# Expert 0's weights split during w_out; ranks, one-hots and slots in other places of TensorE's and VectorE's order

## The chip, the core and the metric

The kernel runs on one core of one Trainium2 chip. The metric is device time in microseconds (us) from the first to the last instruction, with what lies around them. TensorE multiplies; VectorE and ScalarE compute on tiles and empty TensorE's results out of PSUM; POOL (GpSimd) does some element work and issues the indirect transfers; SP issues the plain ones.

## What is computed

One layer of a hybrid trunk on 512 rows of 1024 columns: a norm, three token mixers, an output projection, a norm, then 16 experts in 4 groups, of which each row takes two, and a last norm. The change touches the stretch from the output projection to the first experts:

```
    return y @ w_out                                   # hybrid_mixer
    h = layer_norm(ALPHA * h + mix, ln1_g[l], ln1_b[l])
    ffn = grouped_moe(h, w_router, router_bias, ...)
...
    scores = jax.nn.sigmoid((t @ w_router))            # grouped_moe
    sel = (scores + router_bias).reshape(-1, N_GROUPS, EXPERTS_PER_GROUP)
    g_idx = argmax(sum of the two best sel of each group)
    e_idx = the two best experts of that group
    w_sel = scores at e_idx, divided by their sum
    h = silu(t @ w_gate[e]) * (t @ w_up[e])
    y = sum over a row's experts of w_sel * (h @ w_down[e])
```

## The kernel before

All large products run in three passes: a value is split into a rounded high half and the low half that is left over, and high*high, high*low and low*high are added up in PSUM. `split` makes the two halves of a raw weight page of 128 x 1024: a cast on ScalarE (L316), a subtraction on VectorE (L317). `mm3` (L332 to L334) issues the three products. SBUF is cut into pages of 4 KB per partition; `new` and `drop` take and free them, and a `Ring` hands out a fixed set of pages in turn.

The program is written as one list of instructions; a planner in the framework gives each engine its order by its own estimates. An instruction that is pinned (`pin`, or an engine wrapped as `Pinned`, all of which show as L144) keeps the written order among the pinned ones of its engine. `issue_after(i)` puts an instruction behind `i` on its engine. Engines run their orders strictly in sequence.

**w_out.** The 512 rows are four tiles, n = 0 to 3. Columns 0 to 511 are done for all tiles first; then columns 512 to 1023 tile by tile, TensorE pinned: four units u of six products (`wo_mm`). Between the units stand the router's steps of earlier tiles: transposes and products of `logits`, `scores`, the norm's `moments`, and `rows`, which finishes h1 and stores it to HBM (L1304). `half` adds the product to the residual (L1235) and takes the norm's sums.

**Routing.** `choose(n0, n1)` makes, for two tiles, the mask `Mb` of chosen experts (L1343) with some 20 small VectorE instructions; it returns `weigh`, which makes the routing weights in `rc` (L1355 to L1362). `ranks(n0, n1)` multiplies `Mb` with triangular matrices to get each row's place in its expert's list, adds it into `pos`, and makes the one-hot matrix `oh0` of expert 0 (L1375). `choose(0, 2)`, its `weigh` and `ranks(0, 2)` stand in tile 2 after unit 2; those of tiles 2 and 3 behind tile 3.

**Expert 0's input** is not gathered: `rows0(q, n0, n1)` multiplies tiles n0 to n1 - 1 of the residual with `oh0` into PSUM (L1382); `parts` splits the result. Tile 3 is normed late: a product with `ident` brings x*g into PSUM (L1294), one with the row of means adds the bias (L1295), and ScalarE scales it (L1296).

**Slots.** `slots_of(e0, e1)` makes for each expert a one-hot of 128 x 512 on VectorE (L1461), four products with `rc`, and from them the indices `gidx` and `sidx`; the function it returns (`rest`) makes the weights `wsl` in the same way. Other experts' input comes by an indirect transfer from HBM (`gather`, L1490), is transposed (`ex_in`, L1521) and split (L1513, L1514).

**Experts.** `weights(e)` loads six pages: four units of gate and up (two transfers of 256 KB each, L1504) and two of down (512 KB, L1506). `ex_up` is 24 products of 512 columns in four units, `ex_down` of the expert before follows it: the gate (L1534, L1535), two transposes (L1538), the split `mh` (L1541, L1542), 12 products, and the scatter to HBM (L1551). The split halves lie in rings `whs` and `wls` of three pages each; the raw pages in a ring of all that is free, 31.

Around the change the written order is: w_out's tile 3, `logits(1)`, `scores`, `rows`, `choose(2, 4)`, `rows0(0 and 1, 0, 2)`, `ranks(2, 4)`, the loads of experts 0 and 1, `rows0(0, 2, 4)`, slots of 1, `rows0(1, 2, 4)`, with the splits of expert 0's units 0 to 2 between them (`early`), the gather for expert 1, expert 0's 24 products, `weigh`, the rests, `slots(0)`, `slots(2, 3)`, `slots(4..7)`, `ex_in` of expert 1, its products.

## Time and profile before

| | us |
|---|---|
| median of three timed runs | 903.03 (901.21 to 904.04) |
| the profiled execution | 896.39 |
| its span, first to last instruction | 894.7 |
| TensorE busy in it | 829.8 |
| VectorE, ScalarE, POOL busy | 603.9, 442.9, 169.4 |

The times below are from the start of the span. Line numbers are those of the kernel before; L144 stands for every pinned instruction, which is told apart by its tiles. In a row of the timeline stand start, duration, engine, line, operation, what is written and read, the shape, the count, and in brackets how long the engine had stood idle and what released it. A matmul's duration is modelled and overlaps the next: six products of 512 columns take 1.64 us together, though each is shown with 0.39.

### The profile page before, as it was taken

What the parts mean: (1) busy time and instruction counts of PE and PEld (TensorE: products, weight loads), DVE (VectorE), ACT (ScalarE), POOL (GpSimd) and SP (SyncE); (2) the same over time, 40 slices, a digit from 0 to 9 for tenths busy, and PEclk for the clock granted to TensorE, in tenths of its full rate; (3) what the DMA queues carried; (4) which work ended last, traced back from release to release, by engine and by line L of the source; (5) the groups of instructions that cost most, each with busy time, mean ns of one, the idle gap of its engine ahead of it and who ended that gap; (6) DMA issues with size and microseconds to landing.
All of it is one profiled execution on the core that took longest, in us unless ns stands there. A gap on an engine that the chain in (4) does not pass through costs nothing. (4 is left out here: it accounts for less than half of the span.)

```text
span 894.7 us, 15185 instructions
## 1 busy us (share of the span) xinstructions
PE 829.8 (93%) x5860; PEld 694.0 (78%) x5860; DVE 603.9 (68%) x1104; ACT 442.9 (50%) x824; POOL 169.4 (19%) x197
## 2 busy tenths in 40 slices
PE   8989999999989999999999999999989699999950
PEld 5867778978987999988888888888767577777730
DVE  7775566777666646685834435445467999989958
ACT  6533466654556453556323323333214588888833
POOL 2550001440451330201000000000112122221132
PEclk9989999999999999999999999999999899999985
DMA  6512221022023122144434234247416999997043
GB/s 195 138 53 73 84 71 59 25 78 68 25 96 109 57 71 72 48 144 140 155 105 141 86 103 120 79 156 250 151 47 240 347 354 368 359 356 277 27 168 133
DMA packets 99999, 125.90 MB, mean 141 GB/s; under 512 B 12967, under 2 KB 86775, under 8 KB 99924
## 3 DMA queue, kind: packets, MB, share of 16 engines
q1 hardware_dynamic: 89344, 109.17, 36.7%
q10 hardware_dynamic: 6116, 7.48, 2.6%
q0 software_dynamic: 4464, 8.25, 2.4%
q8 instruction: 47, 0.77, 0.3%
q14 instruction: 28, 0.23, 0.1%
HBM read 118.21 MB, written 14.68 MB: 149 GB/s over the span
## 5 line engine op out<-in xcount | busy, mean ns | idle before, releaser
L317 DVE TENSOR_TENSOR rr<-ff,rr 128x1024 fp32r<-128x1024 f32 x148 | 183.8, 1248 | 115.9 <-ACT rr L316 113.5
L316 ACT CAST rr<-ff 128x1024 fp32r<-128x1024 f32 x150 | 156.9, 1054 | 168.1 <-PE ps L333 126.2
L332 PE MATMUL ps<-rh,rr 128*128 128x512 f32 x384 | 153.8, 400 | 0.0
L333 PE MATMUL ps<-rh,rr 128*128 128x512 f32 x384 | 150.7, 393 | 0.0
L334 PE MATMUL ps<-rh,rr 128*128 128x512 f32 x384 | 150.6, 392 | 0.0
L332 PE MATMUL ps<-rr,rh 128*128 128x256 f32 (+1 forms) x320 | 93.3, 292 | 0.6 <-DVE rh L144 0.6
L334 PE MATMUL ps<-rr,rh 128*128 128x256 f32 (+1 forms) x320 | 91.8, 288 | 0.8 <-issue 0.8
L333 PE MATMUL ps<-rr,rh 128*128 128x256 f32 (+1 forms) x320 | 91.4, 286 | 0.0
L332 PEld LDWEIGHTS ps<-rh,rr 128*128 128x128 f32 x384 | 72.6, 189 | 15.5 <-issue 0.8
L334 PEld LDWEIGHTS ps<-rh,rr 128*128 128x128 f32 x384 | 72.5, 189 | 15.4
L333 PEld LDWEIGHTS ps<-rh,rr 128*128 128x128 f32 x384 | 72.6, 189 | 14.2
L332 PEld LDWEIGHTS ps<-rr,rh 128*128 128x128 f32 x320 | 61.0, 191 | 2.6 <-issue 1.3
L334 PEld LDWEIGHTS ps<-rr,rh 128*128 128x128 f32 x320 | 60.9, 191 | 1.4 <-issue 0.8
L333 PEld LDWEIGHTS ps<-rr,rh 128*128 128x128 f32 x320 | 61.1, 191 | 0.2
L332 PE MATMUL ps<-rr,ro 128*128 128x512 f32 x120 | 48.5, 404 | 0.8 <-ACT ro L1513 0.7
L333 PE MATMUL ps<-rr,ro 128*128 128x512 f32 x120 | 48.3, 402 | 0.8 <-POOL rr L317 0.6
L334 PE MATMUL ps<-rr,ro 128*128 128x512 f32 x120 | 47.7, 398 | 0.6 <-DVE ro L1514 0.6
L1238 POOL TENSOR_TENSOR ff<-ff,ff 128x512 f32<-128x512 f32 x2 | 2.6, 1278 | 213.4 <-DVE ff L144 213.4
L334 PE MATMUL ps<-ro,rr 128*128 128x512 f32 x96 | 37.4, 389 | 0.0
L332 PE MATMUL ps<-ro,rr 128*128 128x512 f32 x96 | 37.3, 389 | 0.0
L333 PE MATMUL ps<-ro,rr 128*128 128x512 f32 x96 | 37.3, 389 | 0.0
L434 DVE SCALAR_TENSOR_TENSOR scr<-ps,vcol,scr 128x511 f32<-128x511 f32 (+2 forms) x36 | 26.7, 743 | 10.7 <-ACT scr L431 10.1
(576 smaller groups left out, 1676.6 us busy)
## 6 DMA issues: line engine op xcount, KB each, us to landing
ff<-in_w_in_dram SPq DMA_DIRECT2D x66, 512.0 KB, 3.4
ff<-in_w_gate_dram SPq DMA_DIRECT2D x47, 256.0 KB, 5.9
ff<-in_w_up_dram SPq DMA_DIRECT2D x47, 256.0 KB, 6.3
ff<-in_w_down_dram SPq DMA_DIRECT2D x19, 512.0 KB, 7.0
fh<-in_w_down_dram SPq DMA_DIRECT2D x10, 512.0 KB, 6.1
ff<-in_w_out_dram SPq DMA_DIRECT2D x8, 512.0 KB, 3.7
fh<-in_w_gate_dram SPq DMA_DIRECT2D x14, 256.0 KB, 6.0
fh<-in_w_up_dram SPq DMA_DIRECT2D x14, 256.0 KB, 7.3
```

The source lines that it names most:

```text
L316: S.copy(a, src)
L317: i = V.tensor_sub(b, src, a.bitcast(F32))
L332: TE.matmul(ps, w(0, k), h(0, k), start=start and k == k0, stop=False)
L333: TE.matmul(ps, w(0, k), h(1, k), start=False, stop=False)
L334: last = TE.matmul(ps, w(1, k), h(0, k), start=False, stop=stop and k == k1 - 1)
L434: V.scalar_tensor_tensor(y[:, sh:], ps[:, :T - sh], convw[:, j, j0:j0 + 1], y[:, sh:], op0=ALU.mult, op1=ALU.add)
L1238: G.tensor_mul(xg3[:, cs], t[:, cs], g1r[:, cs])
```

## The change

Expert 0's weights get six pages of their own and are loaded before the second half of w_out; two of its four units are split there into four new pages (`fr`, taken from the eight pages `fh`). `ranks(0, 2)` moves from tile 2 to tile 3. Behind w_out, `rows0` of tiles 0 and 1 is spread between the router's and the norm's steps of tile 3, which are now all pinned on TensorE. The casts of units 2 and 3 of expert 0 are free to run from `copied` on, their subtractions (`low`) keep the places of two `early`. `slots(2, 3)` and `weigh` go behind unit 2 of expert 0; the rests and `slots(0)` behind unit 1 of expert 1; `slots(4..7)` behind unit 1 of expert 2. The rings of split halves grow from three to five pages each. The functions `wsrc` and `weights` are the same as before, but for the argument `page`.

```diff
@@ -99,7 +99,12 @@
         def __init__(self, n, dt=F32, last=False):
             self.pages = [new((P, D), dt, last=last) for _ in range(n)]
             self.ids = [owner[id(a)][0] for a in self.pages]
-            self.i = 0
+            self.i, self.dt = 0, dt
+
+        def grow(self, n):
+            r = Ring(n, self.dt)
+            self.pages += r.pages
+            self.ids += r.ids
 
         def __call__(self, shape, dt=F32):
             self.i += 1
@@ -1182,7 +1187,8 @@
     branch(2, oB, gB, gla_norm, MB, w_br_b)
     drop(*hT[0], *hT[1])
     rh.close()
-    Pages("fh", 8, F32, side="right")
+    Pages("fr", 4, F32R, side="right")
+    Pages("fh", 4, F32, side="right")
 
 
     def rowload(a):
@@ -1235,7 +1241,7 @@
             W.tensor_add(t[:, cs], t[:, cs], psw)
             W.bn_stats(st[:, c], t[:, cs])
             if n == NT - 1:
-                G.tensor_mul(xg3[:, cs], t[:, cs], g1r[:, cs])
+                act[0] = G.tensor_mul(xg3[:, cs], t[:, cs], g1r[:, cs])
 
         def logits(c):
 
@@ -1243,8 +1249,8 @@
             ps = pst(pm)
             for k in range(4):
                 TE.transpose(ps[:, k * P:(k + 1) * P], t[:, (4 * c + k) * P:(4 * c + k + 1) * P], ident)
-            S.copy(hT1, ps)
-            yield
+            copied = S.copy(hT1, ps)
+            yield copied
             if n == NT - 1:
                 for k in range(4):
                     TE.matmul(psl[c][:, n * E:(n + 1) * E], hT1[:, k * P:(k + 1) * P], gwr[:, 4 * c + k], start=k == 0, stop=k == 3)
@@ -1284,16 +1290,19 @@
                 ms = nr0[:, 0, 0:2]
                 G.tensor_scalar(ms[:, 0:1], nm, 1.0, None, op0=ALU.mult)
                 G.tensor_scalar(ms[:, 1:2], mv[:, 1:2], LN_EPS, r[0], op0=ALU.add, op1=ALU.mult)
+                cs = [slice(c * T, (c + 1) * T) for c in range(2)]
+                psx = [pst(pp) for c in range(2)]
+                for c in range(2):
+                    TE.matmul(psx[c], ident, xg3[:, cs[c]], start=True, stop=False)
+                rows0(0, 1, 2)
                 ps = pst(pm)
                 TE.transpose(ps[:2, :P], ms, ident)
                 mr = sm.tile([P, P], F32, name="mr", tag="sq", bufs=2)[:2]
                 after(lambda: S.copy(mr, ps[:2, :P]))
+                rows0(1, 0, 1)
                 for c in range(2):
-                    cs = slice(c * T, (c + 1) * T)
-                    ps = pst(pp)
-                    TE.matmul(ps, ident, xg3[:, cs], start=True, stop=False)
-                    TE.matmul(ps, mr, gb2[:2, cs], start=False, stop=True)
-                    after(lambda: S.activation(t[:, cs], ps, AF.Copy, scale=r[0]))
+                    TE.matmul(psx[c], mr, gb2[:2, cs[c]], start=False, stop=True)
+                    after(lambda: S.activation(t[:, cs[c]], psx[c], AF.Copy, scale=r[0]))
             elif n:
                 W.scalar_tensor_tensor(t, t, m, g1r, op0=ALU.subtract, op1=ALU.mult)
                 W.scalar_tensor_tensor(t, t, r[0], b1r, op0=ALU.mult, op1=ALU.add)
@@ -1382,6 +1391,22 @@
                 TE.matmul(xps[q][:, c * P:(c + 1) * P], ah[n][:, (4 * q + c) * P:(4 * q + c + 1) * P], oh0[:, n],
                           start=n == 0 and c == 0, stop=n == NT - 1 and c == 3)
 
+    def wsrc(w, e):
+        return w[0, bass.ds(e, 1)].rearrange("o (k p) f -> p (o k) f", p=P)
+
+    def weights(e, page=None):
+
+        r = []
+        for u in range(6):
+            raw = (page or raws)((P, 2, T))
+            if u < 4:
+                for j, w in enumerate((w_gate, w_up)):
+                    nc.sync.dma_start(raw[:, :, 256 * j:256 * j + 256], wsrc(w, e)[:, 2 * u:2 * u + 2])
+            else:
+                nc.sync.dma_start(flat(raw), wsrc(w_down, e)[:, u - 4])
+            r.append(raw)
+        return r
+
     def wo_mm(n, u, w, ps):
         return mm3(ps, pairs(yT, slice(n * P, (n + 1) * P)), lambda b, k: w[b][:, k % 2], 2 * u, 2 * u + 2, u == 0, u == 3)
 
@@ -1398,6 +1423,8 @@
         lns[n][0](0, psw[n])
 
     ws = [wo_unit(1, u) for u in range(2)] + late
+    first = [weights(0, new)]
+    ready = []
     TE = Pinned(nc.tensor)
     for n in range(NT):
         ps = pst(pp)
@@ -1416,21 +1443,25 @@
                 lns[n - 1][3]()
             if u == 2 and n == 2:
                 choose(0, 2, V)()
+            if u == 2 and n == 3:
                 ranks(0, 2, V)
+            if u == 3 and n < 2:
+                ready.append(split(first[0][n], *(new((P, 2, T), F32R, at="fr") for _ in range(2)), pinned=True))
         lns[n][0](1, ps)
-    for _ in lns[3][1](1):
+    half, logits, scores, rows, _ = lns[3]
+    xps += [pst(pp) for _ in range(2)]
+    made = act[0]
+    W, TP = Pinned(V), TE
+    it = logits(1)
+    copied = next(it)
+    rows0(0, 0, 1)
+    for _ in it:
         pass
-    TE = nc.tensor
-    half, logits, scores, rows, _ = lns[3]
     scores()
     rows()
-    xps += [pst(pp) for _ in range(2)]
-    W, TP = Pinned(V), Pinned(nc.tensor)
     weigh = choose(2, 4, W)
-    for q in range(2):
-        rows0(q, 0, 2)
-    TE = TP
     ranks(2, 4, W)
+    rows0(1, 1, 2)
     drop(*x4)
     drop(*yT[0], *yT[1], g1r, b1r)
     for t in (raws, whs, wls):
@@ -1438,10 +1469,14 @@
     ry.close()
     Pages("fl", 8, F32)
     xTs, whs, wls = Ring(4, F32R), Ring(3, F32R), Ring(3, F32R)
+    for p in ready:
+        drop(*p)
+    whs.grow(2)
+    wls.grow(2)
     xgr, yos = Ring(3, last=True), Ring(2, last=True)
     ohp = new((P, 4, NT * P // 2), last=True).bitcast(BF)
     noh = [0]
-    drop(xg3, gb2, ohf, *ah)
+    drop(xg3, gb2, ohf, *first[0], *ah)
     raws = Ring(len(freed[F32]))
 
 
@@ -1481,7 +1516,8 @@
     xgs = []
     for i in range(3):
         t = xgr((P, D))
-        G.memset(t, 0.0)
+        with tc.issue_after(made.ins):
+            G.memset(t, 0.0)
         xgs.append(t)
 
     scats = []
@@ -1491,27 +1527,11 @@
             out=dst, out_offset=None, in_=h1d, in_offset=bass.IndirectOffsetOnAxis(ap=idx, axis=0),
             bounds_check=T - 1, oob_is_err=False)
 
...
 
     def parts(xT, q, ps, V=V):
         qs = slice(4 * q, 4 * q + 4)
         S.copy(flat(xT[0][:, qs]), ps)
-        V.tensor_sub(flat(xT[1][:, qs]), ps, flat(xT[0][:, qs]).bitcast(F32))
+        return V.tensor_sub(flat(xT[1][:, qs]), ps, flat(xT[0][:, qs]).bitcast(F32))
 
     def ex_in(xg):
         xT = [xTs((P, KD, P), F32R), xTs((P, KD, P), F32R)]
@@ -1522,11 +1542,19 @@
             parts(xT, q, ps)
         return xT
 
-    def ex_up(xT, raw, ready=(), e=0):
+    def ex_up(xT, raw, ready=(), e=0, hook={}):
         ps = pst(pp)
         for u in range(4):
-            w = ready[u] if u < len(ready) else split(raw[u], V=G if e == E - 1 and u == 3 else V)
+            if u < len(ready):
+                w = ready[u]
+            elif e == 1:
+                with tc.issue_after(act[0].ins), tc.issue_after(lows.ins):
+                    w = split(raw[u])
+            else:
+                w = split(raw[u], V=G if e == E - 1 and u == 3 else V)
             mm3(ps, lambda b, k: xT[b][:, k], lambda b, k: w[b][:, k % 2], 2 * u, 2 * u + 2, u == 0, u == 3)
+            if u in hook:
+                hook[u]()
         return ps
 
     def ex_down(ps, raw, wcol, sidx_col, m=2 * T, e=0):
@@ -1564,7 +1592,7 @@
 
     def fetch(e):
         wts = weights(e) if e > 1 else first[e]
-        if e % 4 == 1 and e < E - 4:
+        if e % 4 == 1 and 1 < e < E - 4:
             slots_of(e + 3, e + 7)()
         xg = xgs[e % 3]
         if e > 1:
@@ -1572,35 +1600,43 @@
         return wts, ex_in(xg)
 
 
-    first = [weights(0), weights(1)]
+    first.append(weights(1))
     xT = [xTs((P, KD, P), F32R), xTs((P, KD, P), F32R)]
-    ready = []
-
-    def early(u):
-
-        with tc.issue_after(act[0].ins):
-            ready.append(split(first[0][u], pinned=True))
+    for raw in first[0][2:4]:
+        w = whs((P, 2, T), F32R), wls((P, 2, T), F32R)
+        with tc.issue_after(copied.ins):
+            S.copy(w[0], raw)
+        ready.append(w)
+
+    def low(u):
+        W.tensor_sub(ready[u][1], first[0][u], ready[u][0].bitcast(F32))
 
     rows0(0, 2, 4)
-    rest = slots_of(1, 2, W, lambda: early(0))
+    rest = [slots_of(1, 2, W, lambda: low(2))]
     rows0(1, 2, 4)
     parts(xT, 0, xps[0], W)
-    early(1)
     gather(xgs[1], gidx[:, 1:2])
-    parts(xT, 1, xps[1], W)
-    early(2)
+    low(3)
+    lows = parts(xT, 1, xps[1], W)
     wts = first[0]
+
+    def slots23():
+        rest.append(slots_of(2, 4, W))
+        weigh()
+
+    def weights03():
+        with tc.issue_after(lows.ins):
+            rest.append(slots_of(0, 1))
+        for f in rest:
+            f()
+
+    hooks = [{2: slots23}, {1: weights03}, {1: lambda: slots_of(4, 8)()}] + [{}] * (E - 3)
     late = None
     for e in range(E):
         if e == E - 1:
             ex_down(*late, e=e - 1)
         TE = TP if e == 0 else nc.tensor
-        ps = ex_up(xT, wts, ready if e == 0 else (), e=e)
-        if e == 0:
-            weigh()
-            rest()
-            slots_of(0, 1, W)()
-            slots_of(2, 4, W)()
+        ps = ex_up(xT, wts, ready if e == 0 else (), e, hooks[e])
         if 0 < e < E - 1:
             ex_down(*late)
         late = ps, wts, wsl[:, e:e + 1], sidx[:, e:e + 1]
```

## Rows read from the trace of the kernel before

**Rows 1.** Page, part 1: busy us and share of each engine.

```profile
PE 829.8 (93%) x5860; PEld 694.0 (78%) x5860; DVE 603.9 (68%) x1104; ACT 442.9 (50%) x824; POOL 169.4 (19%) x197
```

**Rows 2.** Stage table: length; busy PE, PEld, DVE, ACT, POOL; clock, DMA share, GB/s.

```profile
636.00:642.00 6.00, 6.00 (x34) 4.46 (x32) 0.55 (x1) 1.43 (x3) 1.20 (x1) 1.00 0.00 1
...
658.90:662.10 3.20, 0.05 (x2) 0.06 (x3) 2.63 (x17) 0.63 (x2) 0.00 (x0) 0.97 0.28 114
662.10:666.00 3.90, 3.90 (x18) 3.32 (x19) 2.53 (x14) 0.00 (x0) 0.00 (x0) 0.58 0.01 2
666.00:673.70 7.70, 7.70 (x39) 5.72 (x39) 5.71 (x20) 0.80 (x2) 0.00 (x0) 1.00 0.06 24
673.70:688.50 14.80, 13.21 (x98) 10.23 (x96) 11.07 (x45) 5.84 (x9) 4.83 (x7) 1.00 0.81 283
688.50:694.20 5.70, 5.70 (x28) 4.52 (x28) 5.47 (x9) 3.75 (x4) 1.87 (x1) 1.00 0.64 210
694.20:703.70 9.50, 2.41 (x62) 1.93 (x58) 8.87 (x26) 2.71 (x3) 0.47 (x1) 0.78 1.05 383
703.70:714.40 10.70, 10.70 (x52) 9.07 (x49) 9.53 (x16) 7.19 (x10) 2.94 (x3) 0.88 0.90 323
714.40:724.40 10.00, 10.00 (x51) 8.12 (x50) 9.26 (x11) 8.69 (x13) 2.07 (x2) 1.00 0.98 317
724.40:734.40 10.00, 10.00 (x48) 7.85 (x47) 9.05 (x11) 8.60 (x13) 2.14 (x2) 1.00 1.06 386
734.40:845.00 110.60, 108.11 (x565) 85.78 (x563) 101.94 (x122) 93.16 (x131) 25.84 (x20) 1.00 0.82 292
```

**Rows 3.** Timeline, TensorE in w_out, tile 2 to tile 3.

```profile
662.05 0.20 PE L144 MATMUL ps<-Mb,SUb 128*128 128x16 bf16 x1 [3.15 <-DVE Mb L1343]
...
662.15 2.91 PE L144 MATMUL ps<-ro,ry 128*128 128x512 f32 x6
...
665.90 1.64 PE L144 MATMUL ps<-rr,ry 128*128 128x512 f32 x6
```

**Rows 4.** Timeline, end of w_out to expert 0's products.

```profile
672.03 1.67 PE L144 MATMUL ps<-ro,ry 128*128 128x512 f32 x6
...
681.21 0.19 DVE L144 SCALAR_TENSOR_TENSOR Mb<-scr,ru 128x32 bf16<-128x32 f32 x1
...
683.63 0.20 PE L144 MATMUL ps<-Mb,onb 128*128 128x16 bf16 x2
...
688.48 5.73 PE L144 MATMUL ps<-rr,ro 128*128 128x512 f32 x24
```

**Rows 5.** Timeline, TensorE from expert 0 to expert 1.

```profile
697.43 0.19 PE L144 MATMUL ps<-rc,fl 128*128 128x3 bf16 x2 [3.18 <-DVE rc L144]
...
703.67 1.95 PE L144 MATMUL ps<-ident,fl 128*128 128x128 f32 x8
```

**Rows 6.** Timeline, then line L1490 at 686 to 700: first gather, landing.

```profile
688.12 2.25 POOL L1490 DMA_INDIRECT fl<-h1d,gidx  x1 [9.72 <-DVE ro L144]
...
DMA to landing us min/median/max: 7.6/7.6/7.6
```

**Rows 7.** Page, part 5: VectorE's subtraction of a split.

```profile
L317 DVE TENSOR_TENSOR rr<-ff,rr 128x1024 fp32r<-128x1024 f32 x148 | 183.8, 1248 | 115.9 <-ACT rr L316 113.5
```

**Rows 8.** Timeline, two weight transfers and the last cast; landing of L1506.

```profile
584.03 0.37 SPq L1504 DMA_DIRECT2D ff<-in_w_gate_dram  x1
...
813.66 0.33 SPq L1506 DMA_DIRECT2D ff<-in_w_down_dram  x1
...
856.12 1.05 ACT L316 CAST rr<-ff 128x1024 fp32r<-128x1024 f32 x1 [0.76 <-PE ps L334]
...
DMA to landing us min/median/max: 5.1/6.5/8.0
```

**Rows 9.** Waits, 720 to 862: us in total, times, longest.

```profile
ACT rr L316 <- PE ps L334: 19.7, 39, 1.4
...
PEld ps L332 <- ACT mh L1541: 3.6, 5, 1.4
```

More of the change, by code (lines that the diff above doesn't have):

```diff
@@ L1492, in gather @@
             bounds_check=T - 1, oob_is_err=False)
-    def wsrc(w, e):
-        return w[0, bass.ds(e, 1)].rearrange("o (k p) f -> p (o k) f", p=P)
-    def weights(e):
-        r = []
-        for u in range(6):
-            raw = raws((P, 2, T))
-            if u < 4:
-                for j, w in enumerate((w_gate, w_up)):
-                    nc.sync.dma_start(raw[:, :, 256 * j:256 * j + 256], wsrc(w, e)[:, 2 * u:2 * u + 2])
-            else:
-                nc.sync.dma_start(flat(raw), wsrc(w_down, e)[:, u - 4])
-            r.append(raw)
-        return r
     def parts(xT, q, ps, V=V):
```

## The prediction

> **What bounds the kernel now.** I read the page first: TensorE is busy in 93% of the span [rows 1], so only a stretch in which it stands still can give much. The stage table (busy time in chosen stretches) then shows where that is [rows 2]: apart from the start and the final norm, three stretches around the hand-over from the output projection (w_out) to the experts. From 658.9 to 662.1 TensorE is all but idle; from 662.1 to 666.0 it is busy, but the granted clock is 0.58, most of it the 1.2 GHz level; from 694.2 to 703.7 it works 2.41 of 9.5 us, at 0.78. In the experts (734.4 to 845.0) it is busy 108.11 of 110.6 us at full clock while VectorE is busy 101.94: TensorE sets that pace, VectorE is 8% behind it. The timeline at the stalls says who is waited for. At 662.05 TensorE has waited 3.15 us for `Mb`, the mask that `choose(0, 2)` makes on VectorE, because the small products of `ranks(0, 2)` stand in its pinned order there [rows 3]. At 697.43 it has waited 3.18 us for `rc`, the weights that `weigh` makes [rows 5]; behind that, also pinned, stand the products of `slots(0)`, `slots(2, 3)` and `slots(4..7)`, each behind one-hots on VectorE, and only then the transposes of expert 1, at 703.67 [rows 5]. Between the stalls, from the end of w_out at 673.7 to expert 0's first product at 688.48 [rows 4], TensorE works 13.21 of 14.8 us [rows 2]. I call the end of w_out the origin and count from it.
>
> **Part 1: ranks(0, 2) later.** Their products go from tile 2 to tile 3 of w_out, where `Mb` has been finished for several us. The wait of 3.15 goes. The slow stretch goes with it: six products took 2.91 us at 662.15 against 1.64 at 665.90 [rows 3], 1.27 too much, and eight small ones behind them some 0.3 too much by the same ratio. Together 4.7 us. What is late next is VectorE: from 658.9 to 673.7 it was busy 2.63 + 2.53 + 5.71 = 10.9 us [rows 2], and the stretch shrinks from 14.8 to 10.1. At least 0.8 us of its work doesn't fit and delays something. Bounds: 4.7 if what slips is work that nobody waits for yet (`weigh` of tiles 0 and 1), 1.5 if tile 2's addition, which TensorE's next transposes need, queues behind all of `choose` and `weigh` (some 2 us of waiting come back, and the slow clock with it). I take 3.9.
>
> **Part 2: expert 0's weights.** The load itself gives nothing: these transfers are under way at 584.03 already [rows 8], and from 636 to 642 the queues stand still, at share 0.00, since all free pages are full [rows 2]; the ten issues keep their place on SP's queue, ahead of the stores of h1. What changes is the split of units 0 and 1, done during w_out into four pages of their own. A split costs VectorE 1.25 us [rows 7] and ScalarE a copy. From 636 to 642 VectorE has 5.45 of 6 us free [rows 2], so two subtractions are hidden; if the planner puts them into the full stretch after 658.9 instead, they cost up to 2.5 there. After the origin VectorE has 2 x 1.25 = 2.5 us less to do. The price is pages: the ring of raw weights falls from 31 to 27, with expert 0's six among them.
>
> **Part 3: order between w_out and expert 0.** The products that pick expert 0's rows out of tiles 0 and 1 (`rows0`, 16 in all) are spread into the waits for ScalarE's copies, and `ranks(2, 4)` stands before the last four. The work on TensorE is the same; of the 1.6 us idle there about 0.8 stays (the wait for VectorE's addition after w_out's last product, which the bias product filled before). `Mb` is ready at 681.21 + 0.19, the products of `ranks` ran at 683.63 [rows 4]; by my count of the new order they can start 8.8 us after the origin instead of 9.9, but TensorE, not `Mb`, holds them. Gain 0.8, bounds 0 and 1.6. The zeroing of three gather pages on POOL moves behind the product with g1 and leaves it 0.25 us earlier at most: nothing.
>
> **Part 4: hand-over to expert 1.** `slots(2, 3)`, `weigh`, `slots(0)` and the remainders move into the products of experts 0 and 1, `slots(4..7)` into expert 2. TensorE then goes from expert 0's last product straight to expert 1's transposes and waits for the gather. That was issued 14.4 us after the origin and landed 7.6 later [rows 6]; 0.8 earlier gives 21.2, while the transposes began at 30.0: 8.8 us, part 3 included. The first expert period, 10.7 us at clock 0.88, becomes 10.0 at clock 1.00 [rows 2]: 0.7 more. So TensorE alone could gain 9.5. VectorE doesn't allow it. From 688.5 to 724.4, the end of expert 1, it was busy 5.47 + 8.87 + 9.53 + 9.26 = 33.1 of 35.9 us [rows 2]. The change takes 2.5 out (part 2); the one-hots stay in this stretch, four of them later. 30.6 us at 98% use need 31.3, from a start 0.8 earlier: 5.4 us gained. Pricing the instructions one by one, start to start, gives 7: the next begins a little before the last has ended. I take 6.1, bounds 3.5 (VectorE no fuller than before, 92%) and 9.5. Later experts don't give it back, as TensorE needs 10.0 per expert and VectorE some 9.3.
>
> **Part 5: five split buffers instead of three.** In the experts ScalarE's casts wait 39 times for TensorE to free a buffer, 19.7 us in all [rows 9], but TensorE is idle only 2.5 of 110.6 us there [rows 2]. Between a gain of 2.5 and the loss in the fourth rival, I take nothing.
>
> **Sum.** 3.9 + 6.1 = 10.0 us. The profiled execution took 896.39 us, span 894.7, and becomes 886.4; the same difference off the median of 903.03 (6.6 above the profiled one, 0.7%) gives 893.0.
>
> **Rivals.** First, *the stall in w_out comes back*: part 1 gives 1.5, the sum is 7.6, 895.4. For it: VectorE's 10.9 us in 10.1. Against it: `weigh` can wait.
>
> Second, *TensorE's limit is reached and the deeper buffers help*: 4.7 + 9.5 + 2 = 16.2, 886.8. Against it: VectorE's ledger.
>
> Third, *the experts are bound by transfers*. Four pages fewer, and two loads of expert 4 wait for expert 0's down-projection. If weights set the pace, an earlier start of the experts is given back, and only part 1 stays: 3.9, 899.1. For it: the transfers run at share 0.98 to 1.06 in the first full experts, 317 to 386 GB/s [rows 2]. Against it: the last down-projection is issued at 813.66, lands 5.1 to 8.0 later, and its cast runs at 856.12 [rows 8], over 34 us of lead; four pages are 4/6 of an expert, 7 us, and an earlier start of 10 leaves 17. The Trainium skill speaks for this rival: "DMA: Bandwidth & Descriptors", section "Where 436 GB/s comes from", puts what HBM gives one core at some 358 GB/s. The busiest stretch here shows 386, so the trace doesn't hold that limit exactly, but its neighbourhood is right; by that rule the experts' transfers cannot be sped up, and the sum would be this rival's.
>
> Fourth, slower: *with five buffers the planner issues splits further ahead, and the small copy `mh` of the down-projection stands behind one more cast on ScalarE*. TensorE waits for `mh` only 5 times now, 3.6 us [rows 9]. One cast of 1.05 [rows 8] before each of 15 down-projections costs 15.8, and the sum is 5.8 us slower, 908.8. It decides from 10.0/15 = 0.67 us per expert on. For it: the planner orders by its own estimates and ScalarE runs in order. Against it: ScalarE is busy only 93.16 of 110.6 us [rows 2].
>
> Fifth, *nothing moves*: the gains are there and lost again in other orders of the planner, since all unpinned instructions are planned anew; 903.
>
> **How the numbers follow.** The forecast gets 0.56 (888.5 to 897.5), the first rival 0.13, the second 0.08, the third 0.06, the fourth 0.10, the fifth 0.07. The range takes in the forecast with its bounds, the first, second and third rivals: 886.0 to 899.5; outside are the fourth and the fifth, 0.17. A change of 0.3% (2.7 us) is about what a measurement of this kernel can tell from none: faster 0.83, same 0.07, slower 0.10.
>
> **What would show it.** Part 1: no wait for `Mb` in w_out, clock 1.00 throughout, w_out's end near 669.8; a wait for tile 2's addition would be the first rival. Part 2: two casts and subtractions of expert 0 before the end of w_out. Part 3: expert 0's first product some 14.0 us after that end. Part 4: expert 1's transposes some 21 us after it, with a wait on the gather and no clock loss; VectorE without gaps until expert 3. Part 5: the same period of 10.0 per expert. The prediction is wrong if TensorE waits on weight transfers, if the stretch from w_out's end to expert 3 shrinks by less than 3.5, or if the period per expert rises by over 0.3.

## The result and the profile after

The changed kernel took 887.89 us (median of four runs, 887.66 to 891.75), the kernel before 902.12 in the same series (898.90 to 904.04): ratio 0.9856, interval 0.9815 to 0.9896. A second series (run after2, below) gave 0.9848, interval 0.9814 to 0.9882. Forecast were 893.0 and a range of 886.0 to 899.5: faster, as forecast, and inside the range, 5 us below the forecast and just under the stretch from 888.5 to 897.5 that I gave 0.56. By the ratio the gain is 13.0 us, where 10.0 was forecast. The two profiled executions differ less than the medians, 894.7 against 885.9 us of span; why, the first experiment tells.

Stage table of the changed kernel, with the columns of [rows 2]:

```profile
658.90:662.10 3.20, 3.20 (x18) 2.79 (x19) 2.74 (x14) 0.63 (x2) 0.00 (x0) 1.00 0.29 118
662.10:669.00 6.90, 6.90 (x37) 4.72 (x36) 5.73 (x34) 0.59 (x1) 0.00 (x0) 1.00 0.24 76
669.00:679.00 10.00, 8.39 (x54) 6.01 (x55) 8.06 (x40) 4.07 (x8) 4.43 (x6) 1.00 0.68 234
679.00:685.00 6.00, 6.00 (x43) 5.99 (x43) 3.79 (x9) 1.98 (x3) 0.28 (x1) 0.72 0.82 268
685.00:691.10 6.10, 6.10 (x35) 4.61 (x34) 5.95 (x10) 4.14 (x5) 1.99 (x1) 1.00 0.75 247
691.10:694.20 3.10, 1.85 (x19) 1.47 (x18) 1.93 (x6) 2.49 (x5) 2.23 (x2) 1.00 1.04 383
694.20:706.30 12.10, 10.02 (x55) 7.37 (x55) 11.66 (x26) 7.37 (x10) 0.03 (x1) 1.00 0.99 357
706.30:717.70 11.40, 11.08 (x85) 9.05 (x83) 10.83 (x17) 8.94 (x14) 5.05 (x4) 1.00 1.02 355
```

The two w_out stretches that carried the stall in [rows 2] are now full and at clock 1.00. What is new is the row of 679 to 685: TensorE is busy all the time and the granted clock is 0.72, part of it the 1.2 GHz level. In the timeline the same place reads as follows (line numbers are now those of the changed kernel, L149 stands for every pinned instruction):

```profile
667.36 1.64 PE L149 MATMUL ps<-ro,ry 128*128 128x512 f32 x6
...
668.54 1.28 DVE L1308 SCALAR_TENSOR_TENSOR ff<-ff,rs1o,ff 128x1024 f32<-128x1024 f32 x1
...
669.88 0.68 DVE L149 TENSOR_TENSOR ff<-ff,ps 128x512 f32<-128x512 f32 x1
...
670.61 0.66 PE L149 MATMUL ps<-ident,ff 128*128 128x128 f32 x4 [1.62 <-DVE ff L149]
...
678.61 0.21 PE L149 MATMUL ps<-Mb,onb 128*128 128x16 bf16 x2
...
678.80 4.55 PE L149 MATMUL ps<-ff,ff 128*128 128x128 f32 x24
...
685.08 3.00 PE L149 MATMUL ps<-fr,ro 128*128 128x512 f32 x12
...
692.18 1.09 PE L149 MATMUL ps<-ident,fl 128*128 128x128 f32 x8 [1.05 <-DMA fl<-h1d,gidx]
```

w_out ends at 667.36 + 1.64 = 669.0 (the origin, before 673.7). TensorE then waits 1.62 us, since VectorE runs the 1.28 us pass over tile 2's rows ahead of tile 3's addition. Expert 0 begins 16.1 us after the origin (before 14.8), and at the low clock 24 records of `rows0` products (two records for each) took 4.55 us, where the next 16 took 2.03; the transposes of expert 1 come at 23.2 (before 30.0) and wait for the gather, as forecast. There is no wait for `Mb` and none for `rc`.

The timelines of all profiled executions, cut at the same places (us; w_out counts from the first product of its second half, the next two columns from the end of w_out; the other runs are explained below; medians come from several series, so the text compares ratios):

| run | w_out | expert 0's first product | expert 1's transposes | from there to the last down-projection | rest | median |
|---|---|---|---|---|---|---|
| before | 39.2 | 14.8 | 30.0 | 159.6 | 31.4 | 902.1 |
| before again (k_before) | 41.9 | 14.8 | 30.0 | 161.0 | 32.9 | |
| changed | 34.5 | 16.1 | 23.2 | 160.5 | 33.2 | 887.9 |
| changed again (after2) | 34.6 | 14.5 | 22.2 | 160.7 | 33.2 | 888.2 |
| ranks_only | 34.6 | 20.0 | 35.2 | 159.9 | 32.7 | 898.1 |
| ranks_back | 40.9 | 13.6 | 21.9 | 162.6 | 31.8 | 895.5 |
| order_back | 34.5 | 16.9 | 24.0 | 160.5 | 33.4 | 889.8 |
| hand_back | 34.6 | 14.5 | 29.2 | 157.7 | 32.8 | 892.1 |
| late_split | 34.5 | 15.5 | 23.8 | 162.7 | 35.0 | 891.2 |
| ring3 | 34.5 | 14.5 | 21.4 | 163.5 | 32.1 | 889.6 |
| fill_before | 37.7 | 16.2 | 31.4 | 161.9 | 31.9 | 901.9 |
| fill_after | 34.6 | 14.5 | 22.7 | 162.7 | 33.1 | 888.8 |
| fill_both | 34.6 | 14.5 | 21.7 | 160.0 | 33.3 | 887.5 |
| scatter_first | 34.6 | 14.5 | 21.6 | 165.1 | 32.3 | 892.1 |

The first product itself comes at 634.2 to 638.2, which nothing in these kernels explains: the part ahead of the change varies by that much from one execution to the next.

### The profile page after: what moved, and what is told of

The parts are those of the page before. It is cut to its first block, busy times and chain, and to the rows that moved or that the text cites. A ratio compares the mean times of both kernels' runs of the same rounds, so it can differ in the third digit from the quotient of the medians.

```text
span 885.9 us, 15191 instructions
## 1 busy us (share of the span) xinstructions
PE 825.9 (93%) x5860; PEld 693.5 (78%) x5860; DVE 597.9 (67%) x1104; ACT 442.0 (50%) x824; POOL 170.9 (19%) x197
## 5 line engine op out<-in xcount | busy, mean ns | idle before, releaser
L322 DVE TENSOR_TENSOR rr<-ff,rr 128x1024 fp32r<-128x1024 f32 x125 | 154.6, 1244 | 112.8 <-ACT rr L321 111.5
L321 ACT CAST rr<-ff 128x1024 fp32r<-128x1024 f32 x126 | 132.1, 1053 | 164.7 <-PE ps L338 126.2
L337 PEld LDWEIGHTS ps<-rh,rr 128*128 128x128 f32 x384 | 72.6, 189 | 15.5 <-issue 0.8
L322 DVE TENSOR_TENSOR fr<-ff,fr 128x1024 fp32r<-128x1024 f32 x30 | 36.1, 1218 | 1.4 <-ACT fr L321 1.3
L321 ACT CAST fr<-ff 128x1024 fp32r<-128x1024 f32 x31 | 32.1, 1054 | 6.2 <-PE ps L339 4.6
L1579 POOL DMA_INDIRECT y2d<-fl,sidx x16 | 20.3, 1271 | 69.0 <-ACT fl L1578 32.5
```

The costliest lines, as they stand in the source:

```text
L321: S.copy(a, src)
L322: i = V.tensor_sub(b, src, a.bitcast(F32))
L337: TE.matmul(ps, w(0, k), h(0, k), start=start and k == k0, stop=False)
L1579: s = nc.gpsimd.indirect_dma_start(out=y2d[:m], out_offset=bass.IndirectOffsetOnAxis(ap=sidx_col, axis=0), in_=yo, in_offset=None, bounds_ ...
```

## The experiments

**The same kernels again.** Both kernels unchanged, for a second profile.

> The kernel before, unchanged, for a second profile. The profiled execution of before took 896.4 us and the timed ones 899 to 904, while for the changed kernel both are 887.7; so the profiles show 8.8 us and the medians 14.2. If the before simply varies from run to run, this profile shows where: I expect 896 to 904 us, and if it is near 902, some 5 us more than in the first profile in one place, most likely in the wait between the first two experts or in clock lost there. If it is 896 again, the difference lies between profiled and timed executions and the traces cannot show it.

> The changed kernel, unchanged, for a second profile and a time beside the variants. The two profiles of the kernel before differ by 7.4 us of span with one and the same first wait of 3.15 us; what differs is how long the clock stays at half speed behind it (about 4 us in one, 9 in the other, and again 7.5 against 9 behind the wait between the experts). If that is what makes the medians differ by more than the profiles, the changed kernel, which has only one stretch of 4 us at half speed, should vary less: 886 to 889 us.

Before again took 903.8 us, span 902.1, 7.4 more than its first profile. The stall and the hand-over in its stage table:

```profile
660.70:663.80 3.10, 0.04 (x1) 0.00 (x0) 2.53 (x16) 0.67 (x2) 0.00 (x0) 0.84 0.31 128
663.80:672.60 8.80, 8.71 (x29) 7.32 (x30) 4.30 (x21) 0.49 (x1) 0.00 (x0) 0.50 0.00 1
...
703.90:714.20 10.30, 7.77 (x68) 6.71 (x69) 8.40 (x24) 2.47 (x4) 3.41 (x3) 0.51 1.00 362
```

and in its timeline, TensorE:

```profile
663.89 0.19 PE L144 MATMUL ps<-Mb,SUb 128*128 128x16 bf16 x1 [3.15 <-DVE Mb L1343]
...
663.99 2.91 PE L144 MATMUL ps<-ro,ry 128*128 128x512 f32 x6
...
668.26 2.91 PE L144 MATMUL ps<-rr,ry 128*128 128x512 f32 x6
```

The wait for `Mb` is 3.15 us again, to the hundredth [rows 3]. But behind it the clock stays at the lower level for 8.8 us, where the first profile had some 3.3 (0.58 over 3.9 us [rows 2] is 3.3 at half clock and 0.6 at full); at the hand-over it is 0.51 for 10.3 us, in the first profile 0.78 and 0.88 over two stretches [rows 2]. The 7.4 us are: 1.8 from the start, 2.7 in w_out, 1.4 in the experts, 1.5 behind them. The changed kernel again took 884.8 us of span, median 888.2, with no stretch at the lower clock from w_out to the last expert. So the first pair of profiles is 8.8 us apart and the second 17.3, with the medians (13.0 by 0.9856) between: the stall's price varies, and the profile on which I predicted was one of the cheap ones.

**ranks(0, 2) alone, and everything but it.** The kernel before with part 1 only (ranks_only); the changed kernel without it (ranks_back).

```diff
                 choose(0, 2, V)()
+            if u == 2 and n == 3:
                 ranks(0, 2, V)
```

> The kernel before with one edit: ranks(0, 2) called in tile 3 of w_out instead of tile 2. My theory of part 1: no wait for Mb, clock 1.00 through w_out, its end near 669.8 in the profile instead of 673.7 (the changed kernel: 669.0), so 3.9 us less (bounds 1.5 and 4.7). Of the hand-over nothing moves, so expert 1's transposes come 4 us earlier and no more. Rival 'the stall comes back': 1.5 less. Rival 'later waits swallow it' (the transposes of expert 1 stay at 703.7, since weigh and the one-hots on VectorE set them): 0.

> The changed kernel with ranks(0, 2) back in tile 2 of w_out. Theory: the stall of 3.2 us and the slow clock come back, w_out ends near 673.7, and the time is 3 to 5 us above the changed kernel, some 892. It also tells on the clock after w_out: the changed kernel shows 0.53 and 0.62 in 679 to 683 and its first expert's products come 16.1 us after w_out. If the 1.6 us of waiting for VectorE's addition behind w_out is what that loss follows, here, where VectorE has 3 us more, the wait is 0.8 or less and the clock stays at 1.00: the first product then comes 14 us after w_out, and the total is only 2 us above the changed kernel. If the order of the small products costs the clock, the loss stays.

Alone, the move takes the time to 0.9962 (0.9944 to 0.9981), 3.4 us less; undone in the changed kernel it costs twice that, and more than the 3 to 5 us that I expected: 0.9938 (0.9918 to 0.9958) instead of 0.985, some 7.7 us. The stage table of ranks_only shows what eats the gain there:

```profile
669.00:673.00 4.00, 2.51 (x14) 1.40 (x13) 3.79 (x13) 0.80 (x2) 3.95 (x4) 1.00 0.32 131
673.00:677.00 4.00, 3.99 (x15) 3.09 (x15) 3.33 (x20) 0.47 (x2) 0.50 (x3) 0.57 0.68 242
677.00:680.00 3.00, 3.00 (x13) 1.63 (x13) 1.21 (x8) 0.73 (x2) 0.00 (x0) 1.00 0.81 289
680.00:688.00 8.00, 7.26 (x48) 7.04 (x48) 2.86 (x8) 4.05 (x5) 0.00 (x0) 0.57 0.73 232
```

w_out is 4.7 us shorter, but VectorE is late behind it (3.79 of 4.0 us busy), TensorE is idle 1.5 us there in pieces, and then works twice at the lower clock; expert 0 begins 20.0 us after the origin instead of 14.8, and the whole 4.7 is gone in this execution. The wait in ranks_back, and the stretch at the lower clock behind it:

```profile
663.20 0.18 PE L149 MATMUL ps<-Mb,SUb 128*128 128x16 bf16 x1 [3.15 <-DVE Mb L1352]
```

```profile
664.80:671.70 6.90, 6.90 (x24) 5.84 (x23) 3.72 (x13) 0.59 (x1) 0.00 (x0) 0.51 0.00 0
```

Here w_out took 40.9 us, 6.4 more than in the changed kernel, and some 2 us more are lost in the experts, where the wait for the gather is 2.27 us and the clock is low behind it from 698 to 705. So not all of the 7.7 is the stall in w_out. I had also asked whether the wait for tile 3's addition takes the clock with it. It is 0.78 us long here, and no clock was lost ahead of expert 0; but the next experiments show that a wait of 1.62 mostly costs no clock either.

**The order of part 3.** The changed kernel with the products between w_out and expert 0 as before; the diff shown leaves out the same for those in `rows`.

```diff
...
-    xps += [pst(pp) for _ in range(2)]
     made = act[0]
-    W, TP = Pinned(V), TE
...
-    rows0(0, 0, 1)
...
+    TE = nc.tensor
     scores()
     rows()
+    xps += [pst(pp) for _ in range(2)]
+    W, TP = Pinned(V), Pinned(nc.tensor)
     weigh = choose(2, 4, W)
+    for q in range(2):
+        rows0(q, 0, 2)
+    TE = TP
     ranks(2, 4, W)
-    rows0(1, 1, 2)
```

> The changed kernel with part 3 undone: between w_out and expert 0 the products of rows0 and of xg3 stand as in the kernel before, ranks(2, 4) behind all of rows0 of tiles 0 and 1. In the kernel before with only ranks(0, 2) moved (run ranks_only), expert 0's first product came 20.0 us after w_out, in the kernel before 14.8, in the changed kernel 14.5 or 16.1. Theory 'the order of part 3 is what keeps the gain of part 1': with VectorE late behind a shorter w_out, the old order has several short waits there and the clock falls: first product 16 to 20 us after w_out, time 2 to 5 us above the changed kernel (888). Rival 'part 3 is worth little' (as I predicted it, 0.8): 15 us or less, and the time within 1 us. If the clock falls only in some executions, the profile may show either, and the times decide.

0.9869 (0.9844 to 0.9894): at most a slight loss; the interval covers the changed kernel too. In its profile expert 0's first product comes 16.9 us after the origin, with the clock at 0.59 from 681 to 685. The changed kernel has 16.1 in the profile that lost clock for about as long (679.4 to 682.9), and 14.5 without a loss. Like for like the old order costs 0.8 us, one profile each. That is much less than in ranks_only, and the theory that part 3 saves the gain of part 1 is not shown by the times.

**Is it the wait or the clock?** In both kernels products that nobody reads fill a wait: 14 ahead of `ranks(0, 2)` in the kernel before (fill_before), 7 ahead of the transposes behind w_out in the changed kernel (fill_after).

```diff
+    psf = pst(pm)
+    for _ in range(7):
+        TE.matmul(psf.rearrange("p (a b) -> p a b", b=P), onb, onb[:, None, :].to_broadcast([P, NT, P]), start=True, stop=True)
     it = logits(1)
```

> The kernel before with 14 products of 128x512 (bf16, on a constant, into a PSUM tile that nobody reads) ahead of the products of ranks(0, 2) in w_out: some 3 us of TensorE work in the place where it waits for Mb. The wait for Mb stays as long, TensorE is only busy meanwhile. Theory 'what the stall cost was mostly the clock': no stretch at half speed behind it, w_out ends 2 to 5 us earlier than in the kernel before (673.7 and 678.2 in its two profiles), at some 672, and the time is 1 to 4 us lower. Rival 'the wait itself is the cost': the end of w_out stays at 673.7 or above, and the time at that of the kernel before.

> The changed kernel with 7 such products ahead of the transposes that wait 1.62 us for VectorE's addition behind w_out. The wait stays, TensorE is busy meanwhile. Theory 'the loss of clock in 679 to 683 follows that idle time': the clock stays at 1.00 up to expert 0, its first product comes 14.3 to 14.6 us after w_out instead of 16.1, and the time falls by 1 to 2 us. Rival 'the many small products of 16 and 128 columns bring the clock down': the loss stays at 679 to 683, and the time with it.

TensorE in fill_before:

```profile
662.61 3.19 PE L144 MATMUL ps<-onb 128*128 128x512 bf16 x14
665.83 0.17 PE L144 MATMUL ps<-Mb,SUb 128*128 128x16 bf16 x1
...
665.90 1.62 PE L144 MATMUL ps<-ro,ry 128*128 128x512 f32 x6
...
668.17 1.65 PE L144 MATMUL ps<-rr,ry 128*128 128x512 f32 x6
```

The filler takes as long as the wait did, and the first six products behind it take 1.62 us instead of 2.91: the clock stays, and w_out takes 37.7 us, against 39.2 and 41.9. In the three profiles with the same wait unfilled (before, k_before, ranks_back) some 3 to 9 us at the lower level followed. So the clock is 1.5 to 4.2 us of the stall's price in w_out, the wait itself 3.2 (37.7 against the 34.5 of the changed kernel, which has no wait there). The time followed only a little, 0.9982 (0.9963 to 1.0000), 0 to 3 us: the profile loses the gain again behind w_out (16.2 instead of 14.8, clock 0.50 to 0.74 from 686 to 690) and at the hand-over, where the clock is low for 13 us. It is one profile, so whether the gain in w_out lasts on average is not shown.

fill_after left the time where it was (0.9843, interval 0.9811 to 0.9874). Its clock was at 1.00 up to expert 0, first product 14.5 us after the origin. But so it was in after2, hand_back, ring3, late_split and scatter_first, where the wait of 1.62 stands unfilled; only one profile in six with that wait shows the loss, and 8 us of busy TensorE lie between. My theory for this loss is not shown. The clock was lost elsewhere in fill_after, at the wait for the gather. That wait and the first product of expert 1 behind it, in fill_after:

```profile
692.93 1.48 PE L149 MATMUL ps<-ident,fl 128*128 128x128 f32 x8 [2.21 <-DMA fl<-h1d,gidx]
...
694.81 0.77 PE L337 MATMUL ps<-rr,ro 128*128 128x512 f32 x1
```

and in after2:

```profile
690.92 1.09 PE L149 MATMUL ps<-ident,fl 128*128 128x128 f32 x8 [1.65 <-DMA fl<-h1d,gidx]
...
692.40 0.48 PE L337 MATMUL ps<-rr,ro 128*128 128x512 f32 x1
```

Behind the waits of 2.21, 2.29 (late_split) and 2.27 (ranks_back) that product took 0.77 to 0.78 us instead of 0.48, and the end of expert 1 came 27.8 us after its transposes; behind the waits of 0.93 to 1.65 (the two profiles of the changed kernel, order_back, ring3 and scatter_first) it took 0.47 to 0.48, and the end came 25.3 to 25.7 us after.

**Both waits filled.** The changed kernel with `rows` of tile 2 called behind tile 3's addition, 3 products in the first wait and 6 in the wait for the gather.

```diff
...
+        if e == 1:
+            psf = pst(pm)
+            for _ in range(6):
+                TE.matmul(psf.rearrange("p (a b) -> p a b", b=P), onb, onb[:, None, :].to_broadcast([P, NT, P]), start=True, stop=True)
         return wts, ex_in(xg)
```

> The changed kernel with three edits against lost clock: rows of tile 2 behind tile 3's addition in VectorE's order (they stand in front of it and delay it by 0.8 us), 3 products of 128x512 (bf16, read by nobody) ahead of the transposes that wait for that addition, and 6 ahead of the transposes of expert 1 that wait for the gather. In one profile with the first wait filled (fill_after) the clock was lost after the second, 693 to 700, while expert 1's down-projections came 3 us later against the start; in the two of the changed kernel it was lost after the first wait in one and nowhere in the other. Theory 'idle time at these two places costs clock in some executions': no half speed between w_out and expert 2, time 1 to 2 us below the changed kernel and with less spread. Rival 'VectorE sets the stretch': within 0.5 us, however the clock goes.

887.53 us, 0.9853 (0.9829 to 0.9876), six runs between 886.8 and 888.9: the same as the changed kernel, no better version. Its profile has clock 1.00 from w_out into the experts, but so has after2. The first edit did nothing: the planner put the pass of 1.28 us ahead of the addition again, and that wait is still 1.6 us, 0.95 of it unfilled.

**The hand-over undone** (hand_back): `weigh`, the remainders and the one-hots of `slots` between expert 0 and expert 1 again.

```diff
...
-    hooks = [{2: slots23}, {1: weights03}, {1: lambda: slots_of(4, 8)()}] + [{}] * (E - 3)
+    hooks = [{}] * E
...
+        if e == 0:
+            weigh()
+            rest[0]()
+            slots_of(0, 1, W)()
+            slots_of(2, 4, W)()
```

> The changed kernel with part 4 undone: weigh, the remainders, slots(0) and slots(2, 3) stand again between the products of expert 0 and the transposes of expert 1, slots(4 to 7) again behind the first fetch. Theory: TensorE waits again some 3 us for rc and works through the products at a lower clock; the transposes of expert 1 come some 28 to 30 us after w_out instead of 23.2, and the time is 5 to 9 us above the changed kernel. Rival 'VectorE sets the stretch to expert 1's end anyway': the transposes come later, but the gap closes by the end of expert 1 and the total is within 2 us of the changed kernel.

892.1 us, 0.9908 (0.9882 to 0.9934), some 4 to 5 us above the changed kernel, at the lower end of the 5 to 9 expected. TensorE's waits between the two experts are back, though the one for `rc` is 1.71 us and not some 3:

```profile
691.29 0.19 PE L149 MATMUL ps<-rc,fl 128*128 128x3 bf16 x2 [1.71 <-DVE rc L149]
...
692.34 0.35 PE L149 MATMUL ps<-rc,fl 128*128 128x3 bf16 x8 [0.85 <-DVE fl L149]
...
695.55 0.27 PE L149 MATMUL ps<-rc,fl 128*128 128x3 bf16 x4 [2.86 <-DVE fl L149]
...
698.54 1.95 PE L149 MATMUL ps<-ident,fl 128*128 128x128 f32 x8
```

The transposes come at +29.2 instead of +22.2 to 23.2, and 2.9 of these 6 to 7 us are made up by the last expert (157.7 against 160.6). So the theory holds in its direction, and the rival has its part: almost half of the delay does not last.

**The splits of expert 0 after w_out** (late_split).

```diff
-            if u == 3 and n < 2:
-                ready.append(split(first[0][n], *(new((P, 2, T), F32R, at="fr") for _ in range(2)), pinned=True))
...
     ranks(2, 4, W)
     rows0(1, 1, 2)
+    for n in range(2):
+        ready.append(split(first[0][n], *(new((P, 2, T), F32R, at="fr") for _ in range(2)), pinned=True))
```

> The changed kernel with part 2 undone in what it moves: the casts and subtractions of expert 0's first two weight units stand after w_out (behind ranks(2, 4) in the order) instead of in its tiles 0 and 1; load and pages stay. VectorE gets 2.5 us more in the stretch in which it is full, so by the ledger the experts' end comes 2 to 2.5 us later; expert 0's first product, which needs the first of them, comes later too unless VectorE has a gap ahead of it. Theory: 2 to 3 us above the changed kernel. Rival 'TensorE waits for the gather anyway': within 1 us, only expert 0's products later inside the time until the gather lands.

891.2 us, 0.9886 (0.9859 to 0.9912): 2 to 3 us slower, the size of the 2.5 us of VectorE work, as expected, though the interval overlaps that of the changed kernel. In its profile TensorE waits 0.82 us for a one-hot ahead of expert 0, the gather wait is 2.29, and the clock is lost behind it and once more from 704 to 708, so a part of the price is clock again, and how much of it is VectorE's work is not shown.

**Three split buffers** (ring3).

```diff
-    whs.grow(2)
-    wls.grow(2)
```

> The changed kernel with three split buffers of each kind instead of five in the experts (part 5 undone; the two freed pages stay unused). As I predicted it (part 5 worth nothing): within 1 us of the changed kernel, ScalarE's waits for TensorE back to some 20 us and TensorE's waits for mh back to 4 to 5 us. Rival 'deeper buffers help': 1.5 to 2.5 us slower, with longer expert periods. Rival 'deeper buffers put mh behind casts': 0.5 us or more faster.

889.6 us, 0.9872 (0.9850 to 0.9895). From the end of expert 1 to the end of expert 14 it needs 126.7 us (716.1 to 842.8), the changed kernel 124.4 and 124.6. The kernel before needs 127.3, but does more in it: the eight transposes of expert 3 stand behind this cut, in the other two ahead of it. Its expert 3 begins at 725.74, and from there it is 126.1; the changed kernel, from expert 3's products behind the cut, has 124.6. The kernel before:

```profile
724.38 0.71 PE L1521 MATMUL ps<-ident,fl 128*128 128x128 f32 x5
...
725.74 0.50 PE L332 MATMUL ps<-rr,ro 128*128 128x512 f32 x1
```

The changed kernel:

```profile
713.23 1.04 PE L1541 MATMUL ps<-ident,fl 128*128 128x128 f32 x8
...
717.70 0.39 PE L338 MATMUL ps<-fr,ro 128*128 128x512 f32 x1
```

The waits from 710 to 852 (us in total, times, longest) of the changed kernel:

```profile
ACT rr L321 <- PE ps L339: 9.5, 22, 1.0
...
PEld ps L337 <- ACT mh L1569: 7.7, 13, 1.0
...
ACT fr L321 <- PE ps L339: 6.9, 13, 1.0
```

and of ring3:

```profile
ACT rr L321 <- PE ps L339: 21.0, 37, 1.7
...
PEld ps L337 <- ACT mh L1567: 4.8, 7, 1.4
PEld ps L338 <- DVE rr L322: 3.9, 11, 0.8
...
PEld ps L339 <- DVE ro L1532: 1.7, 3, 1.1
```

The deeper buffers do put `mh` later, 13 waits of 7.7 us instead of 7 of 4.8, which was my slower rival; but they remove the waits for halves of weights and rows (3.9 + 1.7) and a fifth of ScalarE's (9.5 + 6.9 instead of 21.0). On balance they gain 2.3 us in the experts of these profiles, of which the end gives 1.1 back (33.2 against 32.1). By the ratios it is some 1.8, but the intervals overlap, so the times alone do not tell it from nothing.

**The end.** The changed kernel with POOL's subtraction for the last expert's fourth unit behind the scatter of expert 14 (scatter_first).

```diff
-                w = split(raw[u], V=G if e == E - 1 and u == 3 else V)
+                if e == E - 1 and u == 3:
+                    with tc.issue_after(scats[-1].ins):
+                        w = split(raw[u], V=G)
+                else:
+                    w = split(raw[u])
```

> The changed kernel with POOL's subtraction for the last expert's fourth weight unit held behind the issue of expert 14's scatter. In the changed kernel that scatter is issued at 844.65, behind the subtraction, and the loads of y2 that start the final norm wait for it 32 us and are issued only at 848.7, when expert 15 is almost through; in the kernel before they were issued 3.4 us ahead of its end. Theory 'the order on POOL gave back 2 us at the end': 1.5 to 2.3 us less than the changed kernel. Rival 'the end is set by the last scatter and its load in any order': within 0.5 us of it.

892.05 us, 0.9870 (0.9829 to 0.9911): if anything slower, and neither expectation held. The scatter is out earlier and the rest behind the last down-projection is 0.9 us shorter, but expert 15 takes 14.8 us instead of 10.4. VectorE and POOL in scatter_first:

```profile
844.70 6.12 DVE L322 TENSOR_TENSOR rr<-ff,rr 128x1024 fp32r<-128x1024 f32 x1 [2.55 <-ACT rr L321]
844.98 2.41 POOL L322 TENSOR_TENSOR rr<-ff,rr 128x1024 fp32r<-128x1024 f32 x1
...
847.33 2.39 POOL L322 TENSOR_TENSOR fr<-ff,fr 128x1024 fp32r<-128x1024 f32 x1
```

and in the changed kernel:

```profile
842.10 2.41 POOL L322 TENSOR_TENSOR rr<-ff,rr 128x1024 fp32r<-128x1024 f32 x1 [1.90 <-ACT rr L321]
...
843.96 1.62 DVE L322 TENSOR_TENSOR rr<-ff,rr 128x1024 fp32r<-128x1024 f32 x1 [2.53 <-ACT rr L321]
```

With POOL's two subtractions back to back, VectorE's subtraction, 1.25 us otherwise [rows 7], takes 6.12, and everything of expert 15 behind it is late. The first of expert 15's twelve down products comes 2 us later than in the changed kernel. The twelve then take 5.4 us instead of 3.1, since the granted clock is 0.56 from 850 to 857.8, behind a wait of 2.39. So over half of the 4.4 us is clock, and this run does not settle whether POOL's order gave back the 2 us.

## Why the prediction was right, and where not

**What bounds.** Right on the places: the two stalls are gone, and the kernel is faster. But TensorE's 7 us of idle time at the hand-over were not worth 7 us, since VectorE was at work in them (8.87 of 9.5 us [rows 2]); that is part 4.

**Part 1.** The mechanism was right, the term was mis-sized: taken at 3.9, bounds 1.5 to 4.7. w_out shortened by 4.7 us against the profile on which I predicted, the upper bound, by 7.4 against the second, and undoing the move cost 7.7. The step that failed is "six products took 2.91 against 1.64, 1.27 too much, and eight small ones": I took the length of the slow stretch from one execution as a property of the stall. It is some 3 to 9 us behind one and the same wait. The 0.8 us of work that does not fit into VectorE's stretch came as foreseen, but behind w_out: the addition of tile 3 is 0.84 late, 669.88 instead of 669.04, behind the pass over tile 2's rows.

**Part 2.** Not priced by itself; 2.5 us of VectorE work were forecast to leave the full stretch, and late_split costs 2 to 3. The two subtractions ran in w_out, at 634.43 and 649.94, where VectorE had room. The work did go, at least 1.9 of it: from the end of w_out to the end of expert 1 VectorE works 42.4 us, before 44.3.

**Part 3.** Forecast were 14.0 us to expert 0, a gain of 0.8 against the kernel before; it is 14.5 with a steady clock, a gain of 0.3, and 16.1 in the first profile, a loss of 1.3. The step that failed is "about 0.8 stays" of the idle time: 1.62 stays, since the addition is late, and `ranks(2, 4)` starts at +9.6 instead of +8.8. (What had filled that wait before was the product with x*g, L1294, and not the bias product that the prediction names.) Against the old order in this kernel, 16.9, the gain is 0.8 with about the same loss of clock in both; the times (order_back) do not tell it from nothing.

**Part 4.** Transposes forecast at +21.2, found at +23.2 and +22.2, waiting for the gather, as forecast, but the gather was issued 15.7 and 14.4 us after the origin instead of 13.6 and so no earlier than before: part 3's gain did not reach it. The gain of the stretch, forecast at 6.1, is 3.3 us (from the end of w_out to expert 3's products 52.0 before, 48.7 after), in the second profile 4.3: too high. My sign for a wrong prediction was less than 3.5, so the first profile falls just under it and the second does not. By the end of expert 1 it reads as 1.9 and 2.9, but there the changed kernel has already done the transposes of expert 3. The work of VectorE was right (from expert 0's first product to the end of expert 1, 30.6 us forecast; 5.95 + 1.93 + 11.66 + 10.83 = 30.4 measured), "98% use" was not, and it is the step that failed: it is 93%. (30.6 us at 98% are 31.2, not 31.3; nothing hangs on it.) VectorE is 96% busy from 694.2 on, but 1.93 of 3.1 us while the gather is out. The lower bound of 3.5, VectorE no fuller than before, was the nearer one. hand_back gives 4 to 5 by the times.

**Part 5.** Forecast at nothing, between 2.5 and a loss. It is 2.3 us in the experts against ring3, some 1.8 by the times, not clear of noise. "The same period" was wrong: the stretch from expert 3's products to the end of expert 14 took 126.1 us before and 124.6 after. The bound was taken from the wrong row: TensorE's idle time, my 2.5 us, did not shrink at all, its busy time did. Before:

```profile
724.50:851.80 127.30, 123.67 (x638) 97.94 (x637) 116.47 (x138) 107.30 (x152) 28.95 (x23) 1.00 0.79 285
```

After:

```profile
717.90:842.30 124.40, 120.24 (x630) 97.64 (x629) 115.70 (x140) 105.94 (x150) 27.42 (x23) 1.00 0.85 302
```

TensorE is idle for 3.6 us of the first and 4.2 of the second, while it is busy for 3.4 us less; one of these is the set of transposes. The gate and up products took 398 to 402 ns on average before and 390 to 394 after. In ring3 the weight loads wait 3.9 us for low halves where the products themselves wait 0.5, so such waits would stretch products without counting as idle; that this is the whole of it is a reading, not shown.

**The end** was not in the sum. It gave back 1.7 us against the first profile of before and 0.3 against the second; I did not find a cause, and the one I tried fell.

**The sum.** Between the first profiles: part 1 4.7, up to expert 3's products 3.3, from there to the end of expert 14 1.5, expert 15 1.0, the end -1.7: together 8.8, where 10.0 was forecast. That the medians moved by some 13 fits the varying clock of the kernel before, which has two long waits to lose it behind; two profiles do not show its mean. The total thus came out by luck as much as by reasoning: part 1 was too small, part 4 too large, with part 5 beside them. Undone one at a time, parts 1 to 5 cost 7.7, 2 to 3, 1.5, 4 to 5 and 1.8 us by the ratios, 17 to 19 together where the whole is 13.0: the parts are not independent, so none of these is that part's share.

**Rivals.** The stall in w_out did not come back. The second (TensorE's limit, buffers help) has the number nearest to the result, 886.8, but by luck: it was right on the buffers only, and its 9.5 us for the hand-over did not come. Of the third nothing is to be seen: TensorE waits for no weight transfer in the experts, and from 706.3 to 717.7 the transfers run at 355 GB/s. The Trainium skill's 358 GB/s ("DMA: Bandwidth & Descriptors", section "Where 436 GB/s comes from") is near, but 383 was reached at 691 to 694, so the rule did not decide here. The fourth has its mechanism (13 waits for `mh` instead of 7) at 2.9 us over the whole, not 15.8.

## What to carry to other kernels

Price a stall of TensorE as wait plus clock, and take the clock from more than one execution: the wait was 3.15 us each time, the clock behind it cost 1.5 to 4.2. When an engine is moved off the critical path by taking a stall away, look what its neighbour (here VectorE) had been doing meanwhile; the same move was worth 3.4 us alone and 7.7 with the order and the work behind it changed as well. Full use of the next engine is a bound, not an estimate: take the share that the trace shows. And cut two timelines only where both have done the same work; a set of transposes that stands on the other side of a cut moved 1.4 us from one part of this account to another.

## What the runs showed of the hardware

The length of the stretch at 1.2 GHz behind one and the same wait of 3.15 us differs between executions: some 3.3 us (before), 6.9 (ranks_back, where it set in 1.5 us behind the wait's end) and 8.8 (k_before). The Trainium skill says that waits for data let TensorE fall to the lower level, so that the products behind them start slow ("TensorE: Matmul & The Clock Gate", section "HAM oscillation — how this bites in real kernels"); the traces agree (2.91 us for six products in before and k_before, 1.62 with the wait filled). In one profile of the changed kernel the clock fell at 679, when TensorE had been busy since 670.6; five profiles with the same wait of 1.62 ahead kept it, and no run explains the difference.

A subtraction of two SBUF operands on VectorE did not share time with those on POOL, it stood until POOL was through, even where it is recorded as started 0.28 us ahead of POOL's first (844.70 against 844.98 in scatter_first): it ended 1.1 us behind POOL's last one in scatter_first (850.82 against 849.72, and so took 6.12 us) and 1.07 behind it in the changed kernel (845.58 against 844.51, 1.62 us). The Trainium skill calls the port that the two share an exclusive lock and no split of the bandwidth ("Trainium Architecture — The Big Picture", section "What this means for kernel authors"), and these rows agree.
